# A 128-byte unused tile behind the small tiles of the MLP stage, which moves its last sixteen tiles to the remainder of the others

## The chip, the cores and the metric

The kernel runs on one core of one Trainium2 chip. The metric is device time in microseconds (us) of one execution. The kernel before takes 2797.21 us, the median of three runs (2795.43 to 2799.55).

## The reference

One layer of a hybrid decoder over 2048 rows of width 1024, float32 in and out. What is computed:

```python
hn  = rmsnorm(h, norm_mix)
z   = hn @ w_in                                  # split into three groups of heads
mix = concat(s5(z_s5), sparse_attention(z_nsa), rglru(z_lru))
h   = h + mix @ w_out
h   = h + (silu(n @ w_gate) * (n @ w_up)) @ w_down   # n = rmsnorm(h, norm_ffn), D_FF = 22 * 128
return rmsnorm(h, norm_final)
```

The change touches only the line with `w_gate`, `w_up` and `w_down` (the MLP) and the last norm.

## The kernel before

The kernel has three stages one behind the other: the projection and the recurrences (phase_a), the attention and `w_out` (phase_b), and the MLP with the final norm (phase_c and mlp, from line 1665). Every stage has a pool of tiles of its own in SBUF; the pools of phase_b and phase_c lie over each other, and a tile's first writer waits for the last users of what lay in its place.

All large products are made of three matmuls: each float32 operand is split into a high and a low part (`h`, `l` for one operand, `ah`, `al` for the other), and high times high, high times low and low times high are added up in PSUM.

The MLP goes over the rows in two halves of 1024 rows (s = 0, 1). Each half has two parts.

*Gate and up* (`pair`, line 1821): 11 pairs of gate and up blocks. A pair has two column blocks j (gate, up), and for each of them seven products (a Strassen-Winograd scheme: seven products of half size instead of eight). Product n takes its moving operand, 128 x 512 float32 per matmul, from one of seven resident operands, and its weights, 128 x 128, from a pair of tiles `ah`, `al` that `part` (line 1790) writes shortly before. A product is twelve matmuls, each with a weight load of its own (`product`, line 1797):

```python
for k in range(4):
    self.mm(p, w[0][:, k], h[0][:, k], k == 0, False)
    self.mm(p, w[0][:, k], h[1][:, k], False, False)
    self.mm(p, w[1][:, k], h[0][:, k], False, k == 3)
```

The second argument of `mm` is the stationary operand (the weights, loaded ahead of the matmul), the third the moving one, of 512 columns. The trace names the moving operand first: `B<-h,ah`, `B<-l,ah`, `B<-h,al`. The seven operands live in seven *places* 0 to 6, each a tile `h`n and a tile `l`n of 8 KB per partition. Which operand is in which place differs between the halves (line 1681):

```python
PLACE = ({"B11": 0, "T2": 1, "T1": 2, "B21": 3, "T3": 4, "B22": 5, "T4": 6},
         {"B11": 1, "B21": 2, "T2": 3, "T1": 4, "T3": 5, "B22": 6, "T4": 0})
```

From the second pair of a half on, a column block runs the products 1, 6, 5, 2, 7, 3, 4, whose operands are B11, T2, T1, B21, T3, B22, T4. In the first half these are the places 0, 1, 2, 3, 4, 5, 6 in that order, in the second half 1, 3, 4, 2, 5, 6, 0. The first pair of a half goes through each product for both column blocks, and is interleaved with the making of the operands.

*Down* (`fetch` and `piece`, lines 1869 and 1882): the places are used again, for the 22 blocks of the hidden layer: block f takes place f mod 7 of a list `FREED`, with the hidden values in `h`n (the weights here) and `w_down` in `l`n (moving). The blocks come in groups of 4, 3, 3, 3, 3, 3, 3, and each group runs over 16 pieces of output, with three matmuls for each block: 192 matmuls in the first group of a half, 144 in the others. In the first half the groups have the places (0,1,2,3), (4,5,6), (0,1,2), (3,4,5), (6,0,1), (2,3,4), (5,6,0); in the second half (1,3,4,2), (5,6,0), (1,3,4), (2,5,6), (0,1,3), (4,2,5), (6,0,1).

The order of all instructions on each engine is planned on the host (class `Plan`) from fixed costs; addresses do not enter it.

Where the tiles lie: phase_c asks for one placeholder of every name of the list `PC_TAGS` (line 52) in its order (lines 1669 and 1670), and the tiles lie in SBUF in that order. All sizes ahead of `junk` are multiples of 2048 bytes. `junk`, `ms16` and the small `rs_` tiles are 1024 + 128 + 6 x 64 + 6 x 64 = 1920 bytes together. So the tiles behind them, `h0`, `l0`, `h3`, `l3`, six `ah` and six `al`, begin 128 bytes lower in their 2048 bytes than all the large tiles ahead: at remainder 1856, the others at 1984. The list ends 192 bytes below the end of the memory.

Of the kernel before, what the change touches and what calls it, by code (L numbers as in the profile page):

```python
# [51 lines left out]
PC_TAGS = (("gain2", D, 1),) + tuple((f"{x}{n}", 2048, 1) for n in (6, 5) for x in "hl") \  # L52
    + (("raw", D, 4), ("S", 512, 4), ("t3", 512, 1), ("gf0", 512, 1)) + tuple((f"{x}{n}", 2048, 1) for n in (1, 2, 4) for x in "hl") \
    + (("nx", D, 3), ("gf1", 512, 1)) + tuple((n, 512, 2) for n in ("s1", "U2", "U3", "s5", "th")) \
    + (("junk", 256, 1), ("ms16", 32, 1), ("rs_v", 16, 2), ("rs_t", 16, 2), ("rs_a", 16, 2), ("rs_y", 16, 6)) \
    + tuple((f"{x}{n}", 2048, 1) for n in (0, 3) for x in "hl") + (("ah", 512, 6), ("al", 512, 6))
ORDER = (0, 1, 11, 2, 9, 6, 3, 15, 5, 4, 12, 8, 10, 7, 13, 14)
BANKS_A = {"mm": 3, "tr": 3, "lps": 2, "aux": 3, "cacc": 2}
# [2030 lines left out]
```

## Time and profile before

| | |
|---|---|
| median of three runs | 2797.21 us |
| the profiled execution | 2801.13 us, its span 2799.4 us |
| PE (matmul) busy | 2644.0 us, 94% of the span |
| PE weight loads busy | 2145.9 us, 77% |
| VectorE (DVE) busy | 2072.0 us, 74% |
| ScalarE (ACT) busy | 1278.0 us, 46% |
| GpSimd (POOL) busy | 1030.7 us, 37% |
| mean granted TensorE clock | 0.970 |

The span goes from the first to the last instruction of the core; the profiled execution's own time is 1.7 us longer, and 3.9 us above the median of the three runs. Matmuls are pipelined: each one's recorded time overlaps the next one's, so the pace of the PE is read from the starts of its matmuls, not from their durations. The trace gives tiles their names without numbers (`B<-h,ah`); which product a matmul belongs to is found by counting matmuls in the order in which the code issues them. The MLP takes the stretch from 1395 us to the end.

### The profile page before, as it was taken

To read this page: it belongs to the slowest core of one execution; us is meant where nothing else is said; L and a number is where in the kernel's file an instruction comes from. 1 tells how busy PE (TensorE), PEld (TensorE's weight loads), DVE (VectorE), ACT (ScalarE), POOL (GpSimd) and SP (SyncE) were. 2 spreads that over 40 slices of the span, in tenths; PEclk is the share of its full clock that TensorE was granted. 3 is DMA by queue.
4 is the path that set the end of the run, shared out by engine and by line. 5 is a ranking of instruction groups with operands and counts; after the bars stand their busy time and mean duration, and the time that the engine had idled before them with its cause. 6 is when DMAs were issued, how large, how long until landed. Compare 5 with 4: busy or idle time off the path is not lost.

```text
span 2799.4 us, 42394 instructions
## 1 busy us (share of the span) xinstructions
PE 2644.0 (94%) x15153; PEld 2145.9 (77%) x15153; DVE 2072.0 (74%) x4334; ACT 1278.0 (46%) x2725; POOL 1030.7 (37%) x791
## 2 busy tenths in 40 slices
PE   6989989989999999998889999999999999999998
PEld 5756568777887788877668888878887888888886
DVE  8697766269889999999899766665557766665555
ACT  5552433147877778876533333332134333332213
POOL 2445341124444444332356444431106434442112
PEclk9999999979999999999989999999999999999999
DMA  5455556652312121211436222253234222225321
GB/s 169 120 156 161 151 135 199 206 166 54 69 41 63 35 69 35 48 52 33 151 117 229 91 84 89 76 211 105 90 101 133 82 73 86 84 83 196 106 90 60
DMA packets 196562, 301.06 MB, mean 108 GB/s; under 512 B 63136, under 2 KB 111008, under 8 KB 196352
## 3 DMA queue, kind: packets, MB, share of 16 engines
q1 hardware_dynamic: 150320, 264.28, 29.6%
q0 software_dynamic: 43872, 26.22, 4.6%
q10 hardware_dynamic: 2160, 7.87, 0.7%
q8 instruction: 119, 1.95, 0.3%
q14 instruction: 91, 0.75, 0.1%
HBM read 213.70 MB, written 84.61 MB: 107 GB/s over the span
## 4 chain that ended last, share of the span: by engine, by line
PE 69%; DVE 20%; issue 3%; ACT 3%; DMA 3%; POOL 1%; SPq 1%; DVEq 0%; ACTq 0%; POOLq 0%
PE B L206 55%; PE B L397 10%; PE B L1507 3%; DVE l L206 3%; DVE ptl L391 3%; DVE Ps L1410 3%; DVE nx L206 1%; DVE acc L391 1%; DVE Pw L1410 1%; DVE sG L206 1%; DVE sA L206 1%; DVE rs_a L206 1%; DVE h L206 1%; DMA l<-kcS 0%; SPq L206 0%
## 5 line engine op out<-in xcount | busy, mean ns | idle before, releaser
L206 PE MATMUL B<-h,ah 128*128 128x512 f32 x1232 | 488.9, 397 | 9.9 <-ACT h L206 6.9
L206 PE MATMUL B<-l,ah 128*128 128x512 f32 x1232 | 488.2, 396 | 4.3 <-DVE l L206 4.3
L206 PE MATMUL B<-l,h 128*128 128x512 f32 x2112 | 487.4, 392 | 1.6 <-DVE l L206 1.6
L206 PE MATMUL B<-h,al 128*128 128x512 f32 x1232 | 488.2, 396 | 0.0
L206 PEld LDWEIGHTS B<-l,h 128*128 128x128 f32 x2112 | 396.5, 188 | 85.7 <-DVE l L206 2.5
L206 PEld LDWEIGHTS B<-h,ah 128*128 128x128 f32 x1232 | 233.1, 189 | 65.2 <-ACT h L206 7.6
L206 PEld LDWEIGHTS B<-l,ah 128*128 128x128 f32 x1232 | 233.0, 189 | 60.1 <-DVE l L206 5.9
L206 PEld LDWEIGHTS B<-h,al 128*128 128x128 f32 x1232 | 232.8, 189 | 53.5
L391 DVE SCALAR_TENSOR_TENSOR ptl<-B,pth 128x512 f16<-128x512 f32 (+3 forms) x408 | 246.1, 624 | 22.3 <-ACT pth L382 20.5
L206 ACT ACTIVATE ah<-S 128x512 fp32r<-128x512 f32 x176 | 110.7, 630 | 284.1 <-PE B L206 264.0
L382 ACT ACTIVATE pth<-B 128x512 f16<-128x512 f32 (+3 forms) x408 | 214.4, 548 | 55.9 <-PE B L1507 31.6
L397 PE MATMUL B<-wo,mix 128*128 128x512 f32 x768 | 227.1, 412 | 4.6 <-DMA mix<-mixS 3.8
L206 POOL TENSOR_TENSOR al<-S,ah 128x512 fp32r<-128x512 f32 x96 | 143.9, 1500 | 200.3 <-ACT ah L206 194.2
L382 ACT ACTIVATE Ps<-Ps,mn 128x1024 f32<-128x1024 f32 (+7 forms) x192 | 172.7, 902 | 41.3 <-DVE mn L1410 40.1
L397 PE MATMUL B<-KB,Q 128*128 128x384 f32 (+3 forms) x448 | 185.2, 413 | 6.4 <-DVE im L394 2.1
L206 PE MATMUL B<-hnl,wsh 128*128 128x512 f32 x448 | 184.0, 411 | 1.8 <-DVE hnl L206 1.8
L206 PE MATMUL B<-hnh,wsh 128*128 128x512 f32 x448 | 183.7, 411 | 0.5 <-ACT stage L206 0.3
L1507 PE MATMUL B<-ident,Ps 128*128 128x128 f32 x1088 | 181.2, 277 | 1.2 <-ACT Ps L382 0.8
L206 PE MATMUL B<-hnh,wsl 128*128 128x512 f32 x448 | 179.8, 401 | 0.0
L397 PE MATMUL B<-VV,ptl 128*128 128x64 f16 x1448 | 148.2, 195 | 28.4 <-DVE ptl L391 27.5
L206 POOL TENSOR_TENSOR al<-raw,ah 128x512 fp32r<-128x512 f32 x68 | 100.7, 1483 | 194.5 <-ACT ah L206 194.5
L206 POOL TENSOR_TENSOR l<-raw,l 128x1024 fp32r<-128x1024 f32 x22 | 53.9, 2449 | 317.5 <-ACT l L206 309.7
(356 smaller groups left out, 5809.8 us busy)
## 6 DMA issues: line engine op xcount, KB each, us to landing
raw<-in_wgu SPq DMA_DIRECT2D x88, 512.0 KB, 3.6
raw<-gS SPq DMA_DIRECT2D x44, 512.0 KB, 4.4
raw<-in_wd SPq DMA_DIRECT2D x44, 512.0 KB, 4.6
wraw<-in_wzf SPq DMA_DIRECT2D x28, 512.0 KB, 4.5
nx<-in_x SPq DMA_DIRECT2D x24, 512.0 KB, 4.6
gS<-s SPq DMA_DIRECT2D x44, 256.0 KB, 2.0
gS<-U SPq DMA_DIRECT2D x44, 256.0 KB, 2.0
mixS<-out SPq DMA_DIRECT2D x32, 256.0 KB, 4.0
```

The lines of the kernel that those rows point to most:

```text
L206: f(*[real(x) for x in a], **{n: real(x) for n, x in k.items()})
L382: return self.S.activation(o, i, f, **k)
L391: return (eng or self.V).scalar_tensor_tensor(o, a, s, b, op0=op0, op1=op1, **k)
L397: return self.PE.matmul(o, l, r, start=start, stop=stop)
L1410: self.V.tensor_tensor_reduce(out=o, in0=x, in1=b, scale=1.0, scalar=3e38 if first else acc, op0=OP.add, op1=OP.min, accum_out=acc)
L1507: self.PE.transpose(pt.v[:, j - a], P.v[:, c:c + 128], self.ident)
```

## The change

One name more in the list of tiles, `pad`, of 32 float32 values (128 bytes) per partition. Nothing reads or writes it. The sixteen tiles behind it begin 128 bytes higher; the list then ends 64 bytes below the end of the memory.

```diff
-    + (("junk", 256, 1), ("ms16", 32, 1), ("rs_v", 16, 2), ("rs_t", 16, 2), ("rs_a", 16, 2), ("rs_y", 16, 6)) \
+    + (("junk", 256, 1), ("ms16", 32, 1), ("rs_v", 16, 2), ("rs_t", 16, 2), ("rs_a", 16, 2), ("rs_y", 16, 6), ("pad", 32, 1)) \
     + tuple((f"{x}{n}", 2048, 1) for n in (0, 3) for x in "hl") + (("ah", 512, 6), ("al", 512, 6))
```

## Rows read from the trace of the kernel before

**Rows 1.** The page, busy time of each engine over the span (us, share, instructions).

```profile
PE 2644.0 (94%) x15153; PEld 2145.9 (77%) x15153; DVE 2072.0 (74%) x4334; ACT 1278.0 (46%) x2725; POOL 1030.7 (37%) x791
```

**Rows 2.** Busy time by stretch: length, PE, PEld, DVE, ACT, POOL, clock, DMA, GB/s.

```profile
1395.00:1460.00 65.00, 49.77 (x215) 38.27 (x216) 62.76 (x74) 21.83 (x39) 40.35 (x27) 0.80 0.30 101
1460.00:1850.00 390.00, 390.00 (x1686) 316.08 (x1685) 293.76 (x354) 135.06 (x225) 175.48 (x116) 1.00 0.35 117
...
2095.00:2128.00 33.00, 29.22 (x144) 23.77 (x143) 25.53 (x49) 21.49 (x45) 21.38 (x17) 0.95 0.43 144
2130.00:2540.00 410.00, 410.00 (x1772) 332.36 (x1771) 281.60 (x350) 144.61 (x239) 179.61 (x122) 1.00 0.27 90
```

**Rows 3.** Timeline, PE, first half: first matmul of eight consecutive products (start, us).

```profile
1584.51 0.39 PE L206 MATMUL B<-h,ah 128*128 128x512 f32 x1
...
1587.24 0.40 PE L206 MATMUL B<-h,ah 128*128 128x512 f32 x1
...
1590.04 0.40 PE L206 MATMUL B<-h,ah 128*128 128x512 f32 x1
...
1592.84 0.39 PE L206 MATMUL B<-h,ah 128*128 128x512 f32 x1
...
1595.57 0.40 PE L206 MATMUL B<-h,ah 128*128 128x512 f32 x1
...
1598.36 0.40 PE L206 MATMUL B<-h,ah 128*128 128x512 f32 x1
...
1601.16 0.40 PE L206 MATMUL B<-h,ah 128*128 128x512 f32 x1
...
1603.96 0.39 PE L206 MATMUL B<-h,ah 128*128 128x512 f32 x1
```

**Rows 4.** Timeline, PE, second half: first matmul of seven products.

```profile
2129.22 0.39 PE L206 MATMUL B<-h,ah 128*128 128x512 f32 x1
...
2131.97 0.39 PE L206 MATMUL B<-h,ah 128*128 128x512 f32 x1
...
2134.69 0.40 PE L206 MATMUL B<-h,ah 128*128 128x512 f32 x1
...
2159.73 0.39 PE L206 MATMUL B<-h,ah 128*128 128x512 f32 x1
...
2162.46 0.40 PE L206 MATMUL B<-h,ah 128*128 128x512 f32 x1
...
2165.26 0.40 PE L206 MATMUL B<-h,ah 128*128 128x512 f32 x1
...
2168.05 0.40 PE L206 MATMUL B<-h,ah 128*128 128x512 f32 x1
```

**Rows 5.** Timeline, PE, down part: two groups of blocks, each with one matmul before.

```profile
1901.90 33.05 PE L206 MATMUL B<-l,h 128*128 128x512 f32 x145
...
1934.55 33.36 PE L206 MATMUL B<-l,h 128*128 128x512 f32 x145
```

**Rows 6.** Groups by form, MLP: count, busy us, mean ns, idle time before.

```profile
L206 POOL TENSOR_TENSOR al<-S,ah 128x512 fp32r<-128x512 f32 x96 | 143.9, 1500 | 200.3 <-ACT ah L206 194.2 <-issue 3.1 <-PE B L206 2.9
L206 DVE TENSOR_TENSOR U<-B,U 128x512 f32<-128x512 f32 x132 | 89.7, 680 | 7.4 <-PE B L206 6.0 <-POOL U L206 1.2 <-issue 0.2
L206 ACT ACTIVATE ah<-raw 128x512 fp32r<-128x512 f32 x132 | 82.8, 631 | 173.4 <-PE B L206 134.3 <-issue 34.9 <-POOL s L206 2.2
L206 POOL TENSOR_TENSOR s<-U,s 128x512 f32<-128x512 f32 x44 | 66.8, 1519 | 3.3
L206 DVE TENSOR_TENSOR ah<-ah,B 128x512 f32<-128x512 f32 x42 | 28.6, 681 | 7.8 <-PE B L206 7.3
L206 ACT ACTIVATE th<-U 128x512 f32<-128x512 f32 x44 | 27.8, 632 | 36.2 <-DVE U L206 26.6 <-DVE s L206 9.4
```

**Rows 7.** Chain that ended last, hand-over between the halves (start, us, what).

```profile
2089.80 4.82 PE B L206 x21
...
2094.65 0.69 DVE U L206
```

## The prediction

> **What bounds the kernel now.** I read the page's busy times first, then the busy times by stretch, then single matmuls in the timeline. The PE is busy for 2644 of 2799 us, far ahead of every other engine [rows 1], but a busy PE need not be one at its best pace, since recorded matmuls overlap. The table by stretch shows the MLP in two kinds. In 1460 to 1850 and 2130 to 2540 us, the gate and up parts after the start of each half, the PE has no idle microsecond (390.00 of 390, 410.00 of 410) at a granted clock of 1.00, while DVE, the next engine, is busy for 293.76 of 390 and 281.60 of 410 us [rows 2]. There the time is the number of matmuls times their pace. At the start of the MLP, 1395 to 1460 us, it is the other way round: DVE is busy for 62.76 of 65 us and the PE waits; the hand-over between the halves, 2095 to 2128, is mixed [rows 2]. So a change of the PE's pace counts in full in the long stretches, and not at the first start.
>
> The pace is the step of this argument that is easily missed. A product is always twelve matmuls of 128 x 512 with twelve weight loads, the same work each time. Yet the eight starts of rows 3 are 2.73, 2.80, 2.80, 2.73, 2.79, 2.80 and 2.80 us apart. The column block shown runs the places 0 to 6 in order: the two short products are those in places 0 and 3. Place 0 and place 3 are the tiles that lie at remainder 1856, as the weights `ah` and `al` do; the moving operands of the other five lie at 1984. That it is the place and not the product is seen in the second half, where the operands sit elsewhere: the second product of a block (T2, now in place 3) takes 2162.46 - 2159.73 = 2.73 us, and the fourth (B21, 2.73 us before, now in place 2) takes 2168.05 - 2165.26 = 2.79 [rows 3, 4]. And in the first pair of the second half two products in place 3 follow each other: they take 2.75 and 2.72 us [rows 4]. The first of the two still pays for what streamed before it; the second one is the clean case, 2.72 us or 226.7 ns a matmul.
>
> The down part says the same of tiles at 1984 alone. The group of the places 4, 5, 6 (moving and weights both at 1984) takes 33.05 us in its row, the next one with the places 0, 1, 2 and the same number of matmuls 33.36 [rows 5] (each row begins one matmul early). Taking 0.39 us off the first for the last matmul's recorded length, (33.05 - 0.39) / 144 = 226.8 ns: the clean pace again, now at 1984. I read from both that a matmul and the weight load that runs beside it go at 226.7 ns when both operands begin at the same remainder, and at about 233 (2.80 / 12) when they don't.
>
> The Trainium skill speaks against this reading: the page "SBUF — State Buffer", section "Who interferes with whom", gives the PE two independent read ports, one for the moving operand and one for weight loads, and says that "PE and ACT never wait on anyone"; by it no remainder could matter and the sum would be zero. The rows above differ by 0.07 us in 2.8 with nothing else different but the place, so I weigh the trace higher.
>
> **The change, part by part.** No instruction, DMA or queue entry is added, removed or moved: the unused tile has no user, and the order of work is planned without addresses. What moves is sixteen tiles by 128 bytes, and with them all large tiles of the MLP come to 1984.
>
> *Waits at the stage's start.* The moved tiles lie over the attention stage's tiles and wait for their last users. Adding up the sizes of both pools, every moved tile lies over the same attention tiles as before; the nearest border ahead of one is still 416 bytes away. No wait comes or goes: 0.
>
> *The other engines.* If the remainder mattered to DVE, ACT or POOL, operations with a moved tile and an unmoved one, or all moved, would now differ from those with unmoved ones alone. They don't: DVE adds into `ah` in 681 ns and into `U` in 680, ACT writes `ah` in 631 and `th` in 632, POOL makes `al` in 1500 and `s` in 1519 [rows 6]. Bounds: between +1 and -19 ns each, beside a PE that is never waiting in the long stretches. I take 0.
>
> *Gate and up.* A column block takes 1603.96 - 1584.51 = 19.45 us [rows 3]; with all seven products clean it takes 7 x 2.72 = 19.04. That saves 0.41 us, in 10 pairs x 2 blocks x 2 halves = 40 blocks (the second half has the same seven lengths in another order): 16.4 us. A clean product of this part with both operands at 1984 is not seen before. It is bounded by 2.72 us, the shortest product of the trace (the second of two in place 3), and 2.80, as it is now (then nothing is saved here, and the last rival says what is lost). I take 2.72, because the down group at 1984 alone runs at just this pace.
>
> *The first pairs.* In the first half the PE waits for DVE: 0. In the second, the ten products from 2129.22 on and the first of the next pair take 30.51 us until 2159.73 [rows 4], eleven clean ones 29.92; 0.59 less, of which 0.07 is counted above already: 0.5 us.
>
> *Down.* Eleven of the fourteen groups mix places 0 or 3 with others (all but 4,5,6; 2,5,6 and 2,4,5). Each loses 33.36 - 33.05 = 0.31 us today [rows 5]: 3.4 us. Bounds: 0 if the PE waits in them anyway, and 3.6 with 0.31 x 192 / 144 = 0.42 for the two groups of 192 matmuls. I take 3.4.
>
> Sum: 16.4 + 0.5 + 3.4 = 20.3 us. Against the profiled execution's own time (span 2799.4, 1.7 us around it, 2801.1) this gives 2780.8; that execution is 3.9 us above the median of the three runs, which the forecast is set against: 2797.2 - 20.3 = 2776.9, say 2777.
>
> What is late next: nothing in the long stretches. A block of 19.04 us needs DVE for 293.76 / 390 x 19.45 = 14.7 us and POOL for 175.48 / 390 x 19.45 = 8.8 [rows 2], and both have no other limit there. At the hand-over the chain of waits goes from the PE's last products at 2089.80 to DVE at 2094.65 and on through small operations [rows 7]: it starts from the PE's own result, so it moves forward with it.
>
> **The rivals.** *Given back at the hand-over.* If what the second half needs first (operands read back by DMA, turned on the PE, split by ACT and DVE) is paced by DVE's queue and not by the PE's last products, the PE waits longer there and the first half's gain goes: 20 blocks x 0.41 + 6 groups x 0.31 = 10.1 us, so 2777 + 10 = 2787. For it: DVE is busy for 25.53 of 33 us there [rows 2]. Against it: the chain enters that stretch from the PE [rows 7]. Chance 0.07.
>
> *No effect.* The unused tile takes no room in SBUF because nothing uses it, or the two ports are independent after all and places 0 and 3 are quicker for a reason that does not go with the remainder. Then the time stays, 2797. For it: nothing in the program names the tile again. Against it: of the 14 buffers called `ls` in the first stage only four are used, and the ten unused ones keep their room there; and the swap of places between the halves [rows 3, 4] leaves little but the remainder. By the Trainium skill's rule of independent ports, on the page and in the section named above, this would be the outcome. Chance 0.07.
>
> *Slower: the remainder itself is what counts.* In the gate and up part, streams that begin at 1984 are slow beside freshly written weights, whatever these have, and 1856 is the quick one. Then places 0 and 3 turn slow as well: seven products take 7 x 2.80 = 19.6 us instead of 19.45, 0.15 x 40 blocks = 6.0 us more: 2803. It decides from the first product in place 0 after 1460 us. For it: no gate and up product is seen before with both at 1984. Against it: the down group 4, 5, 6 is all at 1984 and quick [rows 5]. Chance 0.04.
>
> **How the numbers follow.** Forecast 0.82, the rivals 0.07, 0.07, 0.04. The forecast's own range is 2773 to 2781: two microseconds of run to run spread either way, as the three runs had, and two more for a wait at a stage's start or a few products less. With the hand-over rival the range goes to 2788; 2773 to 2788 leaves out somewhat more than the last two rivals. A measurement of this kernel tells 0.2%, 5.6 us, from no change. Faster by more: 0.82 + 0.07 = 0.89. Within: 0.07. Slower by more: 0.04 (6.0 us is just over).
>
> **What would show it.** In the new timeline every product after 1460 us is 2.72 us long, those in places 1, 2, 4, 5, 6 as well, a column block 19.04, and all clean down groups are alike at 33.05. The PE stays at 390 of 390 us busy but does more matmuls in it: 390 / 0.2267 = 1720 against 1686 [rows 2]. DVE, ACT and POOL keep their means. Up to 1460 us nothing is different. I am wrong if products in places 1 and 2 still take 2.80 us, if places 0 and 3 join them, or if the PE's wait between the halves grows by as much as the first half gains.

## The result

The changed kernel takes 2778.64 us, the median of four runs (2774.81 to 2784.16), against 2798.38 for the kernel before (four runs, 2795.43 to 2804.34): 19.7 us less, ratio 0.9928 with a 95% interval of 0.9904 to 0.9952. Run again as the control of later experiments it took 2783.18 against 2799.97, 16.8 us less, ratio 0.9943 (0.9930 to 0.9956). The forecast was 2777 in a range of 2773 to 2788. (The kernel before has a fourth run here, hence 2798.38 and not 2797.21.)

The profiled execution has a span of 2782.4 us and a time of 2784.2, the slowest of its four runs, so its trace shows 17.0 us of the gain and not all of it. Where they are can be followed stage by stage. The first product of the MLP starts at 1395.2 us (1395.5 before): nothing is different ahead of it. Each part is measured from its first matmul to the first of the next part, the last one to its last matmul. The first gate and up part takes 452.8 us instead of 461.4, the second 429.8 instead of 438.3. The first down part did not get shorter, 251.6 against 250.8, and the second only by 0.7, 240.9 against 241.6.

The starts of the first, second, third and eighth of the products that [rows 3] show, in the timeline of the changed kernel (start, us, engine):

```profile
1581.41 0.39 PE L206 MATMUL B<-h,ah 128*128 128x512 f32 x1
...
1584.13 0.39 PE L206 MATMUL B<-h,ah 128*128 128x512 f32 x1
...
1586.85 0.39 PE L206 MATMUL B<-h,ah 128*128 128x512 f32 x1
...
1600.45 0.39 PE L206 MATMUL B<-h,ah 128*128 128x512 f32 x1
```

Places 0 and 1 take 2.72 us each, and the seven together 19.04 instead of 19.45. The table by stretch (length, PE, PEld, DVE, ACT, POOL, clock, DMA, GB/s), with the counterparts of [rows 2]:

```profile
1395.00:1460.00 65.00, 49.86 (x217) 38.48 (x218) 62.93 (x74) 21.96 (x40) 40.53 (x27) 0.80 0.31 102
1460.00:1850.00 390.00, 390.00 (x1722) 322.80 (x1721) 307.48 (x357) 137.40 (x228) 178.62 (x119) 1.00 0.37 125
1850.00:1856.00 6.00, 3.98 (x14) 2.90 (x13) 5.93 (x8) 2.44 (x3) 0.75 (x1) 0.87 0.92 277
2088.00:2121.00 33.00, 28.88 (x143) 23.46 (x143) 25.19 (x45) 21.90 (x46) 22.20 (x18) 0.95 0.44 144
```

PE busy time says nothing here: it is 390.00 of 390 us in both kernels. The count in brackets does, 1722 matmuls in those 390 us against 1686. The two groups of the down part, whose rows were 0.31 us apart [rows 5], are now alike (146 matmuls each, one more than there):

```profile
1894.96 33.26 PE L206 MATMUL B<-l,h 128*128 128x512 f32 x146
...
1927.60 33.26 PE L206 MATMUL B<-l,h 128*128 128x512 f32 x146
```

(33.26 - 0.39) / 145 = 226.7 ns. The other engines, to be held against [rows 6] (count, busy us, mean ns, idle before):

```profile
L206 POOL TENSOR_TENSOR al<-S,ah 128x512 fp32r<-128x512 f32 x96 | 143.0, 1492 | 198.1 <-ACT ah L206 195.0 <-issue 3.1
...
L206 ACT ACTIVATE ah<-raw 128x512 fp32r<-128x512 f32 x132 | 82.5, 629 | 163.1 <-PE B L206 127.9 <-issue 34.0 <-DMA raw<-in_wgu 1.2
...
L206 DVE TENSOR_TENSOR ah<-ah,B 128x512 f32<-128x512 f32 x42 | 28.6, 681 | 7.9 <-PE B L206 7.5
```

1492 for 1500, 629 for 631, 681 for 681: these did not change. Two groups not shown did, POOL's `al<-raw,ah` from 1483 to 1406 ns and DVE's from 765 to 789; in the long stretches the PE waits for neither.

What was lost again in this execution is at the change from gate and up to down. The PE's timeline there, changed kernel:

```profile
1847.97 3.11 PE L206 MATMUL B<-l,h 128*128 128x512 f32 x13
1853.09 9.17 PE L206 MATMUL B<-l,h 128*128 128x512 f32 x32 [2.02 <-DVE l L206]
```

the kernel before, and the changed kernel in its control run (after_again):

```profile
1861.12 124.19 PE L206 MATMUL B<-l,h 128*128 128x512 f32 x543 [1.08 <-DVE l L206]
```

```profile
1852.21 53.12 PE L206 MATMUL B<-l,h 128*128 128x512 f32 x233 [1.32 <-DVE l L206]
```

The PE now idles 2.02 us instead of 1.08 for the low part that DVE makes of the fourth block's weights. Behind that wait seven matmuls start 427 ns apart, the pace of the 1.2 GHz level, and the granted clock of 1850 to 1856 is 0.87 in the table above; after the shorter waits of the kernel before and of the control no matmul is slow. At the same place of the second half the idle time goes from 0.57 to 1.51 us, and in the control to 0.7; no matmul is slow there. The chain behind it, changed kernel (start, us, what):

```profile
1830.00 1.60 PE B L206 x7
...
1838.32 6.71 DMA raw<-gS
...
1846.21 0.03 DVE h L206
1846.25 3.27 issue
1849.52 0.69 DVE U L206
...
1851.90 1.15 DVE l L206
...
1853.09 3.12 PE B L206 x9
```

The same DMA in the kernel before and in the control:

```profile
1846.82 6.47 DMA raw<-gS
```

```profile
1838.14 6.01 DMA raw<-gS
```

From the product that starts the chain, through a DMA of 6.71 us and DVE's operations in their order, to the PE's next matmul it is 1853.09 - 1831.60 = 21.5 us; before it was 21.0, and in the control 20.8. The PE's own work from the end of that product to the first matmul of the down part went from 16.8 to 16.4 us, in the control as well. So 0.4 us of the longer wait comes from the quicker products, which leave the PE waiting for a chain that did not get quicker with them; the rest, and the slow matmuls behind it, are this execution's own.

### The profile page after: what moved, and what is told of

Read it like the earlier page. It is cut to its first block, busy times and chain, and to the rows that moved or that the text cites. A ratio compares the mean times of both kernels' runs of the same rounds, so it can differ in the third digit from the quotient of the medians.

```text
span 2782.4 us, 42394 instructions
## 1 busy us (share of the span) xinstructions
PE 2622.0 (94%) x15153; PEld 2145.3 (77%) x15153; DVE 2093.9 (75%) x4334; ACT 1276.7 (46%) x2725; POOL 1026.1 (37%) x791
## 4 chain that ended last, share of the span: by engine, by line
PE 68%; DVE 21%; issue 4%; ACT 3%; DMA 3%; POOL 1%; SPq 1%; DVEq 0%; ACTq 0%; POOLq 0%
PE B L206 54%; PE B L397 10%; DVE l L206 4%; PE B L1507 3%; DVE ptl L391 3%; DVE Ps L1410 3%; DVE acc L391 1%; DVE nx L206 1%; DVE Pw L1410 1%; DMA l<-kcS 1%; DVE sA L206 1%; DVE sG L206 1%; SPq L206 1%; DVE h L206 0%; DMA raw<-gS 0%
## 5 line engine op out<-in xcount | busy, mean ns | idle before, releaser
L206 POOL TENSOR_TENSOR al<-S,ah 128x512 fp32r<-128x512 f32 x96 | 143.0, 1492 | 198.1 <-ACT ah L206 195.0
L397 PE MATMUL B<-VV,pth 128*128 128x128 f16 x1448 | 163.9, 223 | 0.0
```

The lines of the kernel that those rows point to most:

```text
L206: f(*[real(x) for x in a], **{n: real(x) for n, x in k.items()})
L397: return self.PE.matmul(o, l, r, start=start, stop=stop)
```

## Experiments

**e1_reorder: all at one remainder of 512, without an unused tile.** The list on which the chip's memory is laid out is only put in another order:

```diff
-PC_TAGS = (("gain2", D, 1),) + ...
+PC_TAGS = (("ms16", 32, 1), ("rs_v", 16, 2), ("gain2", D, 1)) + ...
-    + (("junk", 256, 1), ("ms16", 32, 1), ..., ("rs_y", 16, 6), ("pad", 32, 1)) \
+    + (("junk", 256, 1), ("rs_t", 16, 2), ("rs_y", 16, 6)) \
-    ... + (("ah", 512, 6), ("al", 512, 6))
+    ... + (("ah", 512, 6), ("al", 512, 6), ("rs_a", 16, 2))
```

> The list of tiles of the MLP is reordered without any unused tile: 256 bytes of small tiles stand ahead of everything, 1536 bytes ahead of the last sixteen tiles, 128 behind them. All large tiles then begin at remainder 192 of 512, but the last sixteen lie 1536 bytes off the others in 2048. Theory A (a matmul and the weight load beside it are quick when moving operand and weights begin at the same remainder of 512): every product 2.72 us, 2779 us like the changed kernel. Rival B (the remainder of 2048 has to agree): places 1, 2, 4, 5, 6 slow at 2.80 and 0, 3 at 2.73 as in the kernel before, about 2797. Rival C (remainder 1984 itself is quick, others are not): all seven places at 2.80, about 2803. Rival D (the 128 bytes more, not where tiles begin, made the difference): 2797, since the total is as before.

Measured: 2780.28 us, ratio 0.9922 (0.9905 to 0.9938), as the changed kernel. Places 0 and 1 in its timeline:

```profile
1581.39 0.39 PE L206 MATMUL B<-h,ah 128*128 128x512 f32 x1
...
1584.11 0.39 PE L206 MATMUL B<-h,ah 128*128 128x512 f32 x1
...
1586.83 0.39 PE L206 MATMUL B<-h,ah 128*128 128x512 f32 x1
```

2.72 us each. The unused bytes as such do nothing (D falls), remainder 1984 is nothing special (C falls), and 1536 bytes between the groups are as good as none (B falls).

**e2_coarse: places at 128, 256 and 512 bytes from the weights.** Small tiles stand ahead of single places:

```diff
+    ... + (("ms16", 32, 1), ("h1", 2048, 1), ("l1", 2048, 1)) \
+    + (("rs_v", 16, 2), ("h2", 2048, 1), ("l2", 2048, 1), ("rs_t", 16, 2), ("rs_a", 16, 2), ("h4", 2048, 1), ("l4", 2048, 1)) \
+    ... + (("junk", 256, 1), ("rs_y", 16, 6), ("pad", 32, 1)) \
```

> The changed kernel with the small tiles spread through the list, so that place 1 lies 128 bytes past the weights' remainder, place 2 256 bytes, place 4 512 bytes, and places 0, 3, 5, 6 and the weights agree. Theory A (remainder of 512): places 1 and 2 at 2.79 to 2.80 us a product, place 4 at 2.72 to 2.73, the rest 2.72 (2.73 behind a slow one); about 6 to 8 us more than the changed kernel. If the remainder of 256 counted, only place 1 is slow; if that of 1024 or 2048 counted, place 4 is slow too; if only 128 to one side matters, place 2 is quick.

Measured (one run): 2785.94 us. Starts of the places 0 to 5:

```profile
1581.37 0.39 PE L207 MATMUL B<-h,ah 128*128 128x512 f32 x1
...
1584.09 0.40 PE L207 MATMUL B<-h,ah 128*128 128x512 f32 x1
...
1586.88 0.39 PE L207 MATMUL B<-h,ah 128*128 128x512 f32 x1
...
1589.61 0.39 PE L207 MATMUL B<-h,ah 128*128 128x512 f32 x1
...
1592.33 0.39 PE L207 MATMUL B<-h,ah 128*128 128x512 f32 x1
...
1595.05 0.39 PE L207 MATMUL B<-h,ah 128*128 128x512 f32 x1
```

Place 1 (128 bytes) takes 2.79 us, place 4 (512) 2.72 as expected. Place 2 (256) takes 2.73 and not 2.79: that is the price of standing behind a slow product. In the second half, where it stands behind a quick one, it takes 2.720. So my modulus was wrong: 256 bytes apart is as good as together. The time is 7 us above the changed kernel's first median, as expected.

**e3_fine: 32, 64 and 96 bytes.**

```diff
+    ... + (("p1", 8, 1), ("h1", 2048, 1), ("l1", 2048, 1)) \
+    + (("p2", 8, 1), ("h2", 2048, 1), ("l2", 2048, 1), ("p3", 8, 1), ("h4", 2048, 1), ("l4", 2048, 1)) \
-    ... ("pad", 32, 1) ...
+    ... ("pad", 8, 1) ...
```

> The changed kernel with unused tiles of 32 bytes ahead of places 1, 2 and 4, so that these lie 32, 64 and 96 bytes past the weights' remainder; the others agree. Theory A in its strict form (any difference counts): all three at 2.79 to 2.80 us a product, 10 to 12 us more than the changed kernel. Rival: what counts is which line of 64 or 128 bytes an operand begins in, so that place 1 (32 bytes off) stays at 2.72 and the price begins at place 2 or 4; or the price grows with the distance in between, 2.74, 2.76, 2.78.

Measured (one run): 2799.98 us, more than was expected. Starts of the places 1, 2, 3, 4, 5:

```profile
1586.17 0.40 PE L207 MATMUL B<-h,ah 128*128 128x512 f32 x1
...
1588.97 0.40 PE L207 MATMUL B<-h,ah 128*128 128x512 f32 x1
...
1591.73 0.39 PE L207 MATMUL B<-h,ah 128*128 128x512 f32 x1
...
1594.47 0.40 PE L207 MATMUL B<-h,ah 128*128 128x512 f32 x1
...
1597.29 0.40 PE L207 MATMUL B<-h,ah 128*128 128x512 f32 x1
```

2.80 us at 32 bytes, 2.76 at 64, 2.82 at 96. No distance of these is free, so the lines of 64 or 128 bytes of the rival fall, and the price does not grow with the distance. Place 3, which agrees with the weights, takes 2.74 us behind place 2, and in the second half, behind place 1, 2.756: here the price of the change is larger than in e2.

**e9_fine2: 160, 192 and 224 bytes.** As e3, with the 128 bytes of `ms16` ahead of `p1`:

```diff
-    ... + (("p1", 8, 1), ("h1", 2048, 1), ("l1", 2048, 1)) \
+    ... + (("ms16", 32, 1), ("p1", 8, 1), ("h1", 2048, 1), ("l1", 2048, 1)) \
```

> The changed kernel with place 1 at 160, place 2 at 192 and place 4 at 224 bytes past the weights' remainder, the others agreeing. Products took 2.803, 2.759 and 2.815 us at 32, 64 and 96 bytes, 2.800 at 128 and 2.720 at 256. Theory A2 (the distance around a ring of 256 bytes counts, either way): 160 as 96, 2.80 to 2.815; 192 as 64, about 2.76; 224 as 32, about 2.80. Rival: only the distance in one direction counts and the price falls from 128 towards 256, so all three lie between 2.72 and 2.80 in falling order.

Measured (one run): 2805.15 us. Starts of the places 1 to 5:

```profile
1589.97 0.40 PE L207 MATMUL B<-h,ah 128*128 128x512 f32 x1
...
1592.78 0.39 PE L207 MATMUL B<-h,ah 128*128 128x512 f32 x1
...
1595.57 0.39 PE L207 MATMUL B<-h,ah 128*128 128x512 f32 x1
...
1598.33 0.40 PE L207 MATMUL B<-h,ah 128*128 128x512 f32 x1
...
1601.13 0.39 PE L207 MATMUL B<-h,ah 128*128 128x512 f32 x1
```

2.81 us at 160 bytes, 2.79 at 192, 2.80 at 224. The falling order of the rival is not there. The ring fits 224 against 32 and, roughly, 160 against 96; it fails for 192 against 64 (2.79, not 2.76). The distances tried, medians over the products of the long stretches, moving operand less weights, modulo 512:

| bytes apart | 0 | 32 | 64 | 96 | 128 | 160 | 192 | 224 | 256 |
|---|---|---|---|---|---|---|---|---|---|
| product, us | 2.720 | 2.803 | 2.759 | 2.815 | 2.792 | 2.806 | 2.790 | 2.802 | 2.720 |

(128 behind a slow product: 2.800. 64 and 192 were seen behind slow products alone. 0 and 256 behind a slow one: 2.734 to 2.763, by what the slow one was. 384, which is e5 below, takes 2.792, as 128.)

**e4_hl: only the low, only the high tile of a place 128 bytes off.**

```diff
+    ... + (("h1", 2048, 1), ("ms16", 32, 1), ("l1", 2048, 1)) \
+    + (("rs_y", 16, 6), ("rs_v", 16, 2), ("h2", 2048, 1), ("rs_t", 16, 2), ("rs_a", 16, 2), ("pad", 32, 1), ("l2", 2048, 1), ...
```

> The changed kernel with the small tiles spread so that in place 1 only the low tile l1 lies 128 bytes off, and in place 2 only the high tile h2; h1, l2 and all else agree (remainder of 512). Theory A (the moving operand of a matmul against the weights loaded beside it): in the products, place 1 pays in its 4 low matmuls of 12 and place 2 in its 8 high ones, so 2.74 to 2.77 and 2.76 to 2.80 us; in the down part, where h is the weights and l the moving operand of one place, all matmuls of places 1 and 2 pay, about 233 ns against 226.7. Rival E (what slows a product is the other engines' writes into ah and al, or the weights' own addresses): places 1 and 2 are either both at 2.72 or both at 2.80, and the down part, whose weights are written long before, stays at 226.7 ns.

Measured (one run): 2790.87 us. Starts of the places 0 to 3:

```profile
1581.59 0.39 PE L207 MATMUL B<-h,ah 128*128 128x512 f32 x1
...
1584.31 0.39 PE L207 MATMUL B<-h,ah 128*128 128x512 f32 x1
...
1587.06 0.40 PE L207 MATMUL B<-h,ah 128*128 128x512 f32 x1
...
1589.81 0.40 PE L207 MATMUL B<-h,ah 128*128 128x512 f32 x1
```

Both places take 2.75 us: in place 1 the four low matmuls start the next one after 234.1 ns and the eight high ones after 226.3 (means inside a product), so a single matmul pays for itself. In place 2, where eight of twelve differ, the eight take 229.8 and the four 227.3; I had expected more. A part of its price falls on the product behind it: place 3, which agrees, takes 2.759 us behind place 2 and 2.720 where it stands behind place 1 (second half). In the down part the group of places 0, 1, 2 takes 33.06 us and that of 4, 5, 6 32.64. Their rows, of 144 matmuls each, 4, 5, 6 first:

```profile
1895.13 32.80 PE L207 MATMUL B<-l,h 128*128 128x512 f32 x144
...
1927.77 33.23 PE L207 MATMUL B<-l,h 128*128 128x512 f32 x144
```

There a moving operand differs from the weights that are loaded next in four of nine matmuls of a piece (l1 twice against h1, l2 twice against h2; l1 agrees with h2, l2 with h0), 64 of 144, so 0.42 / 64 = 6.6 ns each. The weights there were written long before, so rival E falls.

That it is the next weights that count, and not those in use, the kernel before shows more plainly. There `h` and `l` of one place always agree, so by the weights in use no group of the down part would be slow; yet the group 0, 1, 2 is slower than 4, 5, 6 [rows 5]. In its trace the matmul ahead of a step from place 0 to 1 or from 2 to 0 starts the next one after 233 ns and the one behind it after 231, the other five of the nine after 226 to 227.

**e5_weights_only: half of the change.** The unused tile moves only `ah` and `al`:

```diff
-    ..., ("rs_y", 16, 6), ("pad", 32, 1)) \
-    + tuple((f"{x}{n}", 2048, 1) for n in (0, 3) for x in "hl") + (("ah", 512, 6), ("al", 512, 6))
+    ..., ("rs_y", 16, 6)) \
+    + tuple((f"{x}{n}", 2048, 1) for n in (0, 3) for x in "hl") + (("pad", 32, 1), ("ah", 512, 6), ("al", 512, 6))
```

> The unused tile stands behind l3 instead of ahead of h0: only the weights ah and al move by 128 bytes, the places 0 and 3 stay where they were. Theory A: now places 0 and 3 are the slow ones (2.79 us), the product behind each pays 2.735, the others 2.72: a block of 19.21 us against 19.04 and 19.45. The down part stays as in the kernel before. About 10 us more than the changed kernel, 2787 to 2791, ratio 0.996 to 0.997. Rival C (places 0 and 3 are quick by their own address): they stay at 2.72 and nothing is slow, 2781.

Measured: 2791.13 us, ratio 0.9965 (0.9952 to 0.9979). Starts of the places 0, 1, 2, 3, 4:

```profile
1581.52 0.40 PE L206 MATMUL B<-h,ah 128*128 128x512 f32 x1
...
1584.31 0.39 PE L206 MATMUL B<-h,ah 128*128 128x512 f32 x1
...
1587.04 0.39 PE L206 MATMUL B<-h,ah 128*128 128x512 f32 x1
...
1589.76 0.40 PE L206 MATMUL B<-h,ah 128*128 128x512 f32 x1
...
1592.56 0.39 PE L206 MATMUL B<-h,ah 128*128 128x512 f32 x1
```

The time is 0.1 us above the expected range, the ratio inside it. 2.79, 2.73, 2.72, 2.80: the places that were quick before are the slow ones now, at addresses that did not change. Rival C falls a second time.

**after_again: the control.**

> The changed kernel once more, as the control for the three others of this chip: 2777 to 2781 us, ratio 0.993 to the kernel before.

Measured: 2783.18 us (2780.96 to 2789.01), ratio 0.9943 (0.9930 to 0.9956), a little less gain than the first time, and above the 2777 to 2781 expected. The profiled execution, 2780.96 us, is the fastest of the five. In its trace the PE idles 1.3 us at the change to down, not 2.0, and the clock does not fall behind it.

**e7_groups: the fourth block one group later.**

```diff
-GROUPS_D = (4, 3, 3, 3, 3, 3, 3)
+GROUPS_D = (3, 4, 3, 3, 3, 3, 3)
```

> The changed kernel with the first group of the down part three blocks long and the second four (4, 3, 3 becomes 3, 4, 3). Theory: part of the gain was given back at the two changes from gate and up to down, where the PE waits for the fourth block (fetched by DMA when its place and a staging buffer come free, split by ACT and DVE, a chain of some 21 us that does not shorten when the products do); with the block one group later, the PE's waits of 2.4 and 1.9 us and the half clock behind the first go: 3 to 6 us less than the changed kernel, 2773 to 2775. Rival: the wait is for what every first group needs, whichever blocks it has, and stays: within 1 us of the changed kernel.

Measured: 2780.92 us (2772.37 to 2782.05), ratio 0.9925 (0.9911 to 0.9939). At the change to down the PE goes on without a wait:

```profile
1849.40 0.39 PE L206 MATMUL B<-h,al 128*128 128x512 f32 x1
1849.63 55.70 PE L206 MATMUL B<-l,h 128*128 128x512 f32 x245
```

The waits of both halves are gone, which shows what they were for. Counted from the first product to the end the MLP takes 1379.7 us (2776.4 - 1396.8) instead of the control's 1384.3 (2779.2 - 1394.9). Of these 4.6 us 1.6 and 1.0 are in the first two groups of the two halves. The other 1.9 are in the first pair of the second half, 47.2 us instead of 49.1, which the expectation had not named; why that pair got shorter is open. In the whole time the expected 2773 to 2775 is missed and the intervals of the two kernels overlap; a gain of 2 us is not shown by them.

**e6_attn: the same rule for the attention stage.** The long-lived small tiles go to the front, queries, `w_out` and the stage's tiles move by 64 to 128 bytes, so that each moving operand has its weights' remainder of 256:

```diff
         ...
+        self.zero = t([128, 32], "zero")
         self.Q1 = [t([128, 4, 128], f"Q1{k}", F32R) for k in range(QB)]
-        self.zero = t([128, 32], "zero")
+        pool.tile([128, 4, 128], F32R, name="QB", bufs=QB)
+        t([128, 16], "padw")
         self.wo = [t([128, KT, D], f"wo{p}", F32R) for p in range(2)]
+        ...
+        t([128, 16], "padm")
```

> The changed kernel with the tiles of the attention stage laid out so that moving operands and weights of its products begin at the same remainder of 256 (keys and values with queries and probabilities, w_out with its input, the identity with what is turned). If the rule holds there too, its 512-column matmuls of w_out go from 229 to 231 ns to 226.7 and those of the scores from 235: some 1200 matmuls by 3 to 8 ns, 4 to 6 us of PE time. The PE waits there now and then, so 0 to 5 us less than the changed kernel. Rival: the attention stage is paced by the hand-overs between the engines, and nothing of it arrives: within 1 us.

Measured: 2781.54 us (2777.36 to 2783.06), ratio 0.9932 (0.9919 to 0.9944): the control, within the intervals. The products of `w_out`, first in the control, then here (count, busy us, mean ns, idle before):

```profile
L397 PE MATMUL B<-wo,mix 128*128 128x512 f32 x768 | 227.8, 413 | 4.8 <-DMA mix<-mixS 4.0 <-DVE mix L391 0.8
```

```profile
L397 PE MATMUL B<-wo,mix 128*128 128x512 f32 x768 | 228.3, 413 | 5.1 <-DMA mix<-mixS 4.3 <-DVE mix L391 0.8
```

Their median pace stays at 232 to 233 ns. There they come in threes between transposes and narrow matmuls of other operands. The first of a run starts the next one only after some 314 ns in both kernels, and only from the eighth of a run on, in the few long runs, the median goes from 229 to 227. Agreement pays in an unbroken stream.

**e8_both: e6 and e7 together; e10_reorder_groups: e1 and e7 together.**

> Both edits together on the changed kernel: the sum of the two, 3 to 10 us less than the changed kernel if both hold, 2768 to 2775.

> The list of tiles reordered without an unused tile (all large tiles at one remainder of 512) and the first group of the down part three blocks long, the second four. If the two gains add up without the attention stage's layout, it is 2773 to 2779 us, ratio 0.990 to 0.9925; if the layout of the attention stage was part of the best time so far (0.9912), it lies at the ratio of the shorter group alone, 0.9925, or above.

Measured: e8 2775.38 us (2772.26 to 2778.06), ratio 0.9912 (0.9898 to 0.9925); e10 2776.86 (2773.89 to 2778.09), ratio 0.9916 (0.9902 to 0.9929). Both are ahead of the kernel before and, by intervals that do not meet the control's 0.9930 to 0.9956, of the changed kernel as measured there; e10 only just, and against other runs of the kernel before. The intervals do overlap with that of its first measurement (0.9904 to 0.9952) and of e1, which has e10's layout (0.9905 to 0.9938), so in the whole time the gain is shown against one of three measurements alone. e8 misses the 2768 to 2775 expected by 0.4 us, e10 is inside its range. Inside the MLP every trace shows it: from the first product to the end e7, e8 and e10 take 1379.7, 1380.2 and 1380.7 us, the control, e1 and e6 1384.3, 1384.5 and 1385.3. What e8 and e10 are ahead of e7 lies ahead of the MLP, where their first products start at 1392.9 and 1391.3 us instead of 1396.8, and e10 changes nothing there. Since e10 does as well without the attention stage's layout, that is not what made e8's time. e10 needs no unused byte.

## Why the prediction was right

*The pace.* Right, to the hundredth: a clean product 2.72 us, a block 19.04, 1722 matmuls where 1720 were expected, the down groups alike. What had to be inferred, that two operands at 1984 go as well as two at 1856, is shown by the trace after, and e1 and e5 show that it is the agreement and neither address. The reason given, one common remainder, was wider than it need be: in e2 a distance of 256 bytes is as good as none, and in e3 and e9 none of the distances of 32 to 224 bytes tried (seven with e2's 128, in steps of 32) is.

*No instruction, no wait at the stage's start.* Right: counts of instructions are the same, the MLP begins at the same time, and DVE, ACT and POOL keep their means, but for the two groups of `al` named above.

*The sum.* 20.3 us forecast, 19.7 and 16.8 measured in two sets of runs, and 21.2 in e1, which agrees in the same way (2801.52 - 2780.28). The control's median, 2783.18, is above the 2781 of the forecast's own range. So the runs bear out the size to some 3 us, and that the first one came within 2 us of 2777 is in part luck. In the profiled pair the long gate and up parts give 8.6 and 8.5 us, 17.1 where 16.4 + 0.5 were forecast; the first pairs have 0.3 and 0.2 of that, not 0 and 0.5. The down parts were to give 3.4 and gave -0.1 together (0.8 more, 0.7 less). In the control's trace, against the same trace of before, the four parts give 8.5, 8.4, 1.5 and 1.4: there the down parts come to 2.9.

The step that fell short is "what is late next: nothing in the long stretches": I looked for the gain to be given back at the hand-over between the halves, where nothing was lost, and not at the change from gate and up to down inside each half. There a chain of some 21 us stood 1.08 and 0.57 us behind the PE already, visible in the trace of before. What the last products save is waited for there, 0.4 us in the first half. The first group of a half was to take 45.28 - 0.42 and 44.68 - 0.42 us; in the control it took 0.3 more each time (45.14 and 44.56), in the profiled execution 2.6 and 1.1 more (47.45 and 45.33). The difference between the two is a chain that was 0.7 and 0.8 us longer in that execution and, in its first half, the fall of the clock; e7 takes the waits away.

*The rivals.* That unused room would be dropped, and that 1984 itself is slow, are excluded by the trace after; that the hand-over between the halves gives the gain back, by it too: from the last matmul of the first half to the first product of the second it is 0.23 us in both kernels, and the first pair behind it takes 49.05 us instead of 49.25. The Trainium skill's rule of independent read ports ("SBUF — State Buffer", section "Who interferes with whom") would let no remainder matter. In this stream of 128 x 512 matmuls with a weight load each one does: a product takes 2.720 us or 2.803 by nothing but 32 bytes in the address of its moving operand (e3), so here the measurement decides. Whether the two reads meet at a port or behind it, no run shows.

## What to carry to other kernels

Where a stream of matmuls loads new weights for each one, compare the starts of matmuls that do the same work, not their busy time: two paces in one stream point to where the operands lie. Let the moving operand and the weights begin at the same remainder of 256 bytes; the order of the tiles can do that without unused bytes. And when the pace of the busiest engine rises, look at each place where it already waits a little: the chain behind it may not have got shorter.

## What the runs showed of the hardware

With weights loaded beside every 128 x 512 matmul, the pace is 226.7 ns when the moving operand and the weights loaded next begin at the same remainder of 256 bytes and 230 to 235 ns at the other distances tried, and the price is not monotone in the distance: 64 bytes cost less (2.759 us a product) than 32 or 96 (2.803, 2.815), but 192 cost 2.790. Why 64 and 192 differ was not found, nor where the time goes: the recorded length of a weight load is 188 ns at either pace. A product that agrees still pays 0.014 to 0.043 us behind one whose high and low tile, or high tile alone, doesn't. Seven matmuls at the 1.2 GHz pace followed an idle time of 2.02 us of the PE, none one of 1.08, 1.3 or 1.51 us.
